# Log-sum-exp over rows: the early store cut into fifteen transfers of unequal partition counts

## Chip, cores and metric

The kernel runs on one core of a Trainium2 chip. The metric is device time in microseconds (us); the figure for a kernel is the median of its runs.

## The reference

```python
def setup_inputs():
    batch, seq, dim = 32, 512, 1024
    return {"x": np.random.randn(batch, seq, dim).astype(np.float32)}

def reference(x):
    max_x = np.max(x, axis=-1, keepdims=True)
    return (max_x.squeeze(-1) + np.log(np.sum(np.exp(x - max_x), axis=-1))).astype(np.float32)
```

There are 16,384 rows of 1024 floats, 64 MB to be read, and one float per row, 64 KB, to be written.

## The kernel before

Each of the 128 partitions takes 128 rows of x, so the results form a tile `res` of 128 partitions by `NC` = 128 columns. The first `W` = 112 columns hold one block of the output (`out_rows`, 112 consecutive floats of each partition), the last `B` = 16 columns another (`out_rest`). The kernel takes the logarithm of the plain sum of exponentials without subtracting the maximum, and checks beside that that no sum went out of bounds; only if one did, a repair branch computes everything again with the maximum. With this input the branch isn't taken.

Eighteen loads, listed in `LOADS` from 16 rows per partition down to less than half a row, go into a ring of 48 rows per partition. They are issued on SyncE (SP) by `load` (L140), in order; SP waits before a load until the engines have let go of its part of the ring. All loads are issued well before the kernel's end, since the last ones find free space early. ScalarE (ACT) computes the exponentials of what has landed, in place (L230); the sums are formed on VectorE (DVE) (L241), on GpSimd (POOL) and DVE together (L235 and L172), or with a fused multiply-add of half rows near the end (L251). The last row comes in two pieces, whose sums ACT accumulates itself (L204).

When the first `LATE` = 119 rows per partition are summed, ACT computes the logarithm of the first 112 columns (`ln_early`, L270), between two of its exponentials. SP waits for that and issues the early store of these 112 columns (L278): one transfer of 128 partitions with 448 bytes each. It raises the semaphore `sp.sem`, called `early_store`, by 16 when it has landed.

After the last exponential, ACT computes the logarithm of the other 16 columns (L281, and L283 for the last one, which is `ln_last`). SP waits for it and issues the last store (L287), 128 partitions with 64 bytes each, on the semaphore `stored`. Beside these, DVE and TensorE (PE) finish the check (L292 to L310). At the end SP waits for `done`, which ACT and DVE raise after the check, then for the early store (L368) and for the last store (the instruction behind L369), and clears the semaphores. So the order on SP at the end is: wait for L270, early store, wait for L283, last store, waits for the end.

A transfer raises its semaphore by 16 in all. Transfers issued on SP stand in one queue, called q1 in the profile.

Of the kernel before, what the change touches and what calls it, by code (L numbers as in the profile page):

```python
# [16 lines left out]
B = 16  # L17
LATE = 119
AHEAD = 3

# [31 lines left out]
def kernel(  # L54
# [5 lines left out]
    nc = tc.nc  # L60
# [4 lines left out]
    P = nc.NUM_PARTITIONS  # L65
# [11 lines left out]
    W = NC - B  # L77
# [4 lines left out]
    out_rows = out_flat[0 : P * W].rearrange("(p c) -> p c", p=P)  # L82
    out_rest = out_flat[P * W : n].rearrange("(p c) -> p c", p=P)

    def source(e0, size):
        assert e0 >= W * d or e0 + size <= W * d
        return x_rest[:, e0 - W * d : e0 - W * d + size] if e0 >= W * d else x_rows[:, e0 : e0 + size]
# [8 lines left out]
    def sbuf(name, cols, dtype=fp32, rows=P):  # L96
        return nc.alloc_sbuf_tensor(name, [rows, cols], dtype).ap()
# [3 lines left out]
    res = sbuf("res", NC)  # L101
# [18 lines left out]
    sp = Counted(nc, nc.sync, "early_store")  # L120
# [14 lines left out]
    def load(i, here, done_before, size):  # L135
        for a, b, who, at in users:
            if a < here + size and b > here:
                sp.wait(who, at)
        users[:] = [u for u in users if not (u[0] < here + size and u[1] > here)]
        return nc.sync.dma_start(  # L140
            out=ring[:, here : here + size], in_=source(done_before, size)
        ).then_inc(landed[i], 16)
# [44 lines left out]
    for i, (size, ops) in enumerate(loads):  # L187
# [5 lines left out]
        dma = load(i, here, done_before, size)  # L193
        if i < AHEAD:
            first_loads.append(dma.ins)
# [3 lines left out]
        for k, (how, s) in enumerate(ops):  # L199
            rows = ring[:, p : p + s * d].rearrange("p (c d) -> p c d", d=d)  # L200
            if how in "YZ":
# [3 lines left out]
                    out=last_exp[:, here - p : end - p], in_=ring[:, here:end], func=AF.Exp,  # L205
# [10 lines left out]
            elif how == "A":  # L216
# [3 lines left out]
                    out=v, in_=v, func=AF.Exp, accum_out=sumexp[:, c : c + 1]  # L220
# [11 lines left out]
            if how == "F":  # L232
# [3 lines left out]
                    out=rows[:, :, 0:H], in0=rows[:, :, 0:H], in1=rows[:, :, H:d], op=ALU.add  # L236
                ))
                folded.append((c, s, p, at))
            elif how == "R":
                dve.wait(act, at)  # L240
                who = (dve, dve.did(nc.vector.reduce_sum(  # L241
                    out=sumexp[:, c : c + s], in_=rows, axis=AX.X
                )))
                users.append((p, p + s * d, *who))
            elif how == "T":
# [3 lines left out]
                for r in range(s):  # L249
                    lo = rows[:, r, 0:H]  # L250
                    who = (dve, dve.did(nc.vector.scalar_tensor_tensor(  # L251
                        out=lo, in0=lo, scalar=1.0, in1=rows[:, r, H:d],
# [13 lines left out]
            if c == LATE:  # L266
# [4 lines left out]
                    out=res[:, 0:W], in_=sumexp[:, 0:W], func=AF.Ln  # L271
# [3 lines left out]
                early_act = summed_by_act  # L275
        assert here == end
    sp.wait(act, ln_early)
    nc.sync.dma_start(out=out_rows, in_=res[:, 0:W]).then_inc(sp.sem, 16)  # L278

    act.wait(dve, dve.n)  # L280
    act.did(nc.scalar.activation(out=res[:, W:LAST], in_=sumexp[:, W:LAST], func=AF.Ln))  # L281
# [2 lines left out]
        out=res[:, LAST:NC], in_=last_sum, func=AF.Ln, bias=sumexp[:, LAST:NC]  # L284
# [8 lines left out]
        out=clamped[:, LATE:NC], in0=sumexp[:, LATE:NC], scalar=LOW,  # L293
# [10 lines left out]
        out=over[:, 0:half], in0=last_piece[:, 0:half], scalar=CEILING,  # L304
# [15 lines left out]
            read.then_inc(done, 1)  # L320
    with nc.If(all_fine < 1):

        nc.scalar.wait_ge(sp.sem, 16)
        nc.scalar.wait_ge(stored, 16)
        rows = 0
        steps = 0
        for c0 in range(0, NC, RING):
            s = min(RING, NC - c0)
            v = ring[:, 0 : s * d].rearrange("p (c d) -> p c d", d=d)
            neg = clamped[:, c0 : c0 + s]  # L330
            if c0:
                nc.scalar.wait_ge(ready, steps)
            edge = max(c0, min(W, c0 + s))
            for c1, c2 in ((c0, edge), (edge, c0 + s)):
                if c1 == c2:
                    continue
                nc.scalar.dma_start(
                    out=ring[:, (c1 - c0) * d : (c2 - c0) * d],
                    in_=source(c1 * d, (c2 - c1) * d),
                ).then_inc(again, 16)  # L340
                rows += 16
            nc.vector.wait_ge(again, rows)
            nc.vector.tensor_reduce(
                out=neg, in_=v, op=ALU.max, axis=AX.X, negate=True
            ).then_inc(ready, 1)
            nc.vector.wait_ge(ready, steps + 1)
            nc.vector.tensor_add(
                out=v, in0=v, in1=neg[:, :, None].to_broadcast([P, s, d])
            ).then_inc(ready, 1)
            nc.scalar.wait_ge(ready, steps + 2)  # L350
            nc.scalar.activation(out=v, in_=v, func=AF.Exp).then_inc(ready, 1)
            nc.vector.wait_ge(ready, steps + 3)
            nc.vector.reduce_sum(
                out=sumexp[:, c0 : c0 + s], in_=v, axis=AX.X
            ).then_inc(ready, 1)
            steps += 4
        nc.scalar.wait_ge(ready, steps)
        nc.scalar.activation(out=res, in_=sumexp[:, 0:NC], func=AF.Ln).then_inc(ready, 1)
        nc.vector.wait_ge(ready, steps + 1)
        nc.vector.tensor_sub(out=res, in0=res, in1=clamped).then_inc(ready, 1)  # L360
        nc.scalar.wait_ge(ready, steps + 2)
        nc.scalar.dma_start(out=out_rest, in_=res[:, W:NC]).then_inc(again, 16)
        nc.scalar.dma_start(out=out_rows, in_=res[:, 0:W]).then_inc(again, 16)
        nc.scalar.wait_ge(again, rows + 32)

    nc.scalar.sem_inc(done, 1)
    nc.sync.wait_ge(done, 2)
    nc.sync.wait_ge(sp.sem, 16)  # L368
    nc.sync.sem_clear(range(landed[0].num, stored.num))  # L369
    kind = dict(sync_type="semaphore", id=stored.num, ant_name="stored")  # L370
    nc.sync.add_instruction(mybir.InstEventSemaphore(
# [54 lines left out]
```

## Time and profile before

| | |
|---|---|
| time, median of 3 runs | 161.67 us (161.55 to 161.7) |
| span of the profiled execution | 160.2 us |
| the difference of the two | 1.47 us |
| DVE busy | 114.2 us, 71% of the span |
| ACT busy | 114.5 us, 71% |
| POOL busy | 37.3 us, 23% |
| PE busy | 2.2 us, 1% |
| q1's packets | 97.8% of 16 engines' span |
| read from HBM, written to it | 67.11 MB, 0.07 MB |

The profile records one execution, and only its span; the time of a run also holds what lies before the span's first instruction and behind its last. Busy time doesn't count waiting, nor the issuing of DMAs, which shows only in SP's rows of the timeline (marked SPq). A row of the timeline has the start and the length in us, the engine, the line and the operation with its output and input. The span starts with the first load's issue.

### The profile page before, as it was taken

What the parts mean: (1) busy time and instruction counts of PE and PEld (TensorE: products, weight loads), DVE (VectorE), ACT (ScalarE), POOL (GpSimd) and SP (SyncE); (2) the same over time, 40 slices, a digit from 0 to 9 for tenths busy, and PEclk for the clock granted to TensorE, in tenths of its full rate; (3) what the DMA queues carried; (4) which work ended last, traced back from release to release, by engine and by line L of the source; (5) the groups of instructions that cost most, each with busy time, mean ns of one, the idle gap of its engine ahead of it and who ended that gap; (6) DMA issues with size and microseconds to landing.
All of it is one profiled execution on the core that took longest, in us unless ns stands there. A gap on an engine that the chain in (4) does not pass through costs nothing.

```text
span 160.2 us, 219 instructions
## 1 busy us (share of the span) xinstructions
PE 2.2 (1%) x26; PEld 1.1 (1%) x26; DVE 114.2 (71%) x59; ACT 114.5 (71%) x31; POOL 37.3 (23%) x11
## 2 busy tenths in 40 slices
PE   0000000000000000000000000000000000000022
PEld 0000000000000000000000000000000000000011
DVE  0000000009999499994999859959999999999996
ACT  3000059990799709995099949992999989799996
POOL 0000000000000000000000994690004969891000
DMA  7996996996996996996999999999999999999992
GB/s 262 524 524 262 524 524 262 524 524 262 524 524 262 524 507 278 524 491 295 483 442 442 442 425 409 409 409 471 423 405 426 458 409 393 450 413 425 411 411 102
DMA packets 2881, 67.18 MB, mean 419 GB/s; under 512 B 576, under 2 KB 704, under 8 KB 1344
## 3 DMA queue, kind: packets, MB, share of 16 engines
q1 hardware_dynamic: 2880, 67.18, 97.8%
q14 instruction: 1, 0.01, 0.0%
HBM read 67.11 MB, written 0.07 MB: 419 GB/s over the span
## 4 chain that ended last, share of the span: by engine, by line
DMA 52%; ACT 28%; DVE 19%; issue 1%; SPq 0%; PE 0%
DMA ring<-in_x_dram 52%; ACT ring L230 28%; DVE sumexp L241 16%; DVE sumexp L172 2%; DVE ring L251 1%; SPq L140 0%; DVE over L303 0%; PE count L308 0%; ACT res L270 0%; DVE clamped L292 0%; DVE fine L310 0%; DVE sumexp L214 0%
## 5 line engine op out<-in xcount | busy, mean ns | idle before, releaser
L230 ACT ACTIVATE ring<-ring 128x16384 f32<-128x16384 f32 (+16 forms) x23 | 111.7, 4909 | 41.9 <-DMA ring<-in_x_dram 41.9
L241 DVE TENSOR_REDUCE sumexp<-ring 128x16 f32<-128x16384 f32 (+4 forms) x9 | 85.6, 9512 | 41.6 <-ACT ring L230 41.6
L235 POOL TENSOR_TENSOR ring<-ring 128x3072 f32<-128x3072 f32 (+3 forms) x7 | 37.1, 5311 | 107.2 <-ACT ring L230 107.2
L172 DVE TENSOR_REDUCE sumexp<-ring 128x6 f32<-128x3072 f32 (+3 forms) x7 | 18.4, 2655 | 0.0
L251 DVE SCALAR_TENSOR_TENSOR ring<-ring 128x512 f32<-128x512 f32 x15 | 9.6, 688 | 0.4 <-ACT ring L230 0.4
L126 ACT ACT_TABLE_LOAD x1 | 1.3, 1283 | 2.4 <-PEq L63 2.4
L157 PE MATMUL count<-far,bad 128*1 128x1 f32 x2 | 0.2, 164 | 153.0 <-DVE clamped L152 153.0
L127 DVE MEMSET ones<- 128x1 f32 x1 | 0.1, 59 | 2.5 <-PEq L63 2.5
L161 PE MATMUL count<-sumexp,ones 128*1 128x1 f32 x18 | 1.6, 164 | 3.6 <-DVE ring L251 3.6
L251 DVE DVE_READ_ACCUMULATOR ring<-ring 128x1 f32 x15 | 1.2, 83 | 0.0
L204 ACT ACTIVATE last_exp<-ring 128x544 f32<-128x544 f32 (+1 forms) x2 | 1.2, 585 | 0.0
L157 PEld LDWEIGHTS count<-far,bad 128*1 128x1 f32 x2 | 0.1, 80 | 153.0 <-DVE clamped L152 153.0
L161 PEld LDWEIGHTS count<-sumexp,ones 128*1 128x1 f32 x18 | 0.8, 81 | 4.5 <-DVE ring L251 4.5
L303 DVE SCALAR_TENSOR_TENSOR over<-ring 128x240 f32<-128x240 f32 x1 | 0.4, 404 | 0.0
L310 DVE TENSOR_SCALAR fine<-count 1x1 int32<-1x1 f32 x1 | 0.1, 146 | 0.3 <-PE count L308 0.3
L152 DVE SCALAR_TENSOR_TENSOR clamped<-clamped,sumexp 128x119 f32<-128x119 f32 x1 | 0.3, 282 | 0.0
L270 ACT ACTIVATE res<-sumexp 128x112 f32<-128x112 f32 x1 | 0.3, 279 | 0.0
L283 ACT ACTIVATE res<-last_sum,sumexp 128x1 f32<-128x1 f32 x1 | 0.3, 261 | 0.0
L204 ACT ACTIVATION_READ_ACCUMULATOR last_exp<-ring 128x1 f32 x2 | 0.3, 126 | 0.0
L147 DVE TENSOR_SCALAR clamped<-sumexp 128x119 f32<-128x119 f32 x1 | 0.2, 221 | 0.0
L281 ACT ACTIVATE res<-sumexp 128x15 f32<-128x15 f32 x1 | 0.2, 208 | 0.0
L292 DVE SCALAR_TENSOR_TENSOR clamped<-sumexp 128x9 f32<-128x9 f32 x1 | 0.2, 169 | 0.0
(17 smaller groups left out, 1.8 us busy)
## 6 DMA issues: line engine op xcount, KB each, us to landing
ring<-in_x_dram SPq DMA_DIRECT2D x1, 6912.0 KB, 23.9
ring<-in_x_dram SPq DMA_DIRECT2D x1, 6400.0 KB, 19.7
ring<-in_x_dram SPq DMA_DIRECT2D x1, 4608.0 KB, 15.9
ring<-in_x_dram SPq DMA_DIRECT2D x1, 3584.0 KB, 24.0
ring<-in_x_dram SPq DMA_DIRECT2D x1, 3072.0 KB, 19.1
ring<-in_x_dram SPq DMA_DIRECT2D x1, 2288.0 KB, 24.1
ring<-in_x_dram SPq DMA_DIRECT2D x1, 1664.0 KB, 20.9
ring<-in_x_dram SPq DMA_DIRECT2D x1, 1264.0 KB, 23.6
```

What stands on the lines that cost most here:

```text
L126: nc.scalar.preload_act_table_set("natural_log_exp_and_others")
L152: dve.did(nc.vector.scalar_tensor_tensor(out=clamped[:, 0:LATE], in0=clamped[:, 0:LATE], scalar=0.0, in1=sumexp[:, 0:LATE], op0=ALU.bypass ...
L157: pe.did(nc.tensor.matmul(count, lhsT=bad[:, 0:1], rhs=far, start=True, stop=False))
L161: return pe.did(nc.tensor.matmul(count, lhsT=ones, rhs=sumexp[:, c : c + 1], **kw))
L172: at = dve.did(nc.vector.reduce_sum(out=sumexp[:, c0 : c0 + s0], in_=halves, axis=AX.X))
L204: at = act.did(nc.scalar.activation(out=last_exp[:, here - p : end - p], in_=ring[:, here:end], func=AF.Exp, accum_out=first_sum if how == ...
L230: at = act.did(nc.scalar.activation(out=v, in_=v, func=AF.Exp))
L235: at = pool.did(nc.gpsimd.tensor_tensor(out=rows[:, :, 0:H], in0=rows[:, :, 0:H], in1=rows[:, :, H:d], op=ALU.add))
L241: who = (dve, dve.did(nc.vector.reduce_sum(out=sumexp[:, c : c + s], in_=rows, axis=AX.X)))
L251: who = (dve, dve.did(nc.vector.scalar_tensor_tensor(out=lo, in0=lo, scalar=1.0, in1=rows[:, r, H:d], op0=ALU.mult, op1=ALU.add, accum_out ...
L270: ln_early = act.did(nc.scalar.activation(out=res[:, 0:W], in_=sumexp[:, 0:W], func=AF.Ln))
L303: dve.did(nc.vector.scalar_tensor_tensor(out=over[:, 0:half], in0=last_piece[:, 0:half], scalar=CEILING, in1=last_piece[:, half : 2 * half ...
```

## The change

The early store is issued as fifteen transfers in a row, over 15, 14, 13 and so on down to 2 partitions, which makes 119, and over the last 9. Each carries the 448 bytes of each of its partitions and raises `sp.sem` by 16, so that the two waits for the early store count to 240. Nothing else differs.

```diff
+PIECES = (15, 14, 13, 12, 11, 10, 9, 8, 7, 6, 5, 4, 3, 2, 9)
...
     sp.wait(act, ln_early)
-    nc.sync.dma_start(out=out_rows, in_=res[:, 0:W]).then_inc(sp.sem, 16)
+    edge = 0
+    for size in PIECES:
+        nc.sync.dma_start(
+            out=out_rows[edge : edge + size], in_=res[edge : edge + size, 0:W]
+        ).then_inc(sp.sem, 16)
+        edge += size
+    assert edge == P
...
-        nc.scalar.wait_ge(sp.sem, 16)
+        nc.scalar.wait_ge(sp.sem, 16 * len(PIECES))
...
-    nc.sync.wait_ge(sp.sem, 16)
+    nc.sync.wait_ge(sp.sem, 16 * len(PIECES))
```

## The prediction

> **What bounds the kernel now.** I read the page's first lines and its chain of waits, then SP's own rows in the timeline (SP carries both stores), then what SP waits for, and then the DMA issues.
>
> ```profile
> span 160.2 us, 219 instructions
> DMA 52%; ACT 28%; DVE 19%; issue 1%; SPq 0%; PE 0%
> ```
>
> Loading, exponentials and sums alternate along the whole span; SP's issuing is 0% of the chain. So the change, which adds nothing but DMA issues on SP after the last load was issued, can act only at the very end, through the store that follows it there.
>
> ```profile
> 136.82 2.23 SPq L140 DMA_DIRECT2D ring<-in_x_dram  x1
> 150.28 0.28 ACT L270 ACTIVATE res<-sumexp 128x112 f32<-128x112 f32 x1
> 150.59 0.35 SPq L278 DMA_DIRECT2D out_dram<-res  x1
> 158.48 0.26 ACT L283 ACTIVATE res<-last_sum,sumexp 128x1 f32<-128x1 f32 x1
> 158.77 0.34 SPq L287 DMA_DIRECT2D out_dram<-res  x1
> 158.95 0.15 DVE L310 TENSOR_SCALAR fine<-count 1x1 int32<-1x1 f32 x1 [0.28 <-PE count L308]
> ...
> SPq L278 <- ACT res L270: 11.5, 1, 11.5
> SPq L287 <- ACT res L283: 7.8, 1, 7.8
> ...
> out_dram<-res SPq DMA_DIRECT2D x1, 56.0 KB, 7.4
> out_dram<-res SPq DMA_DIRECT2D x1, 8.0 KB, 1.4
> ```
>
> Columns are start, us, engine and line; below them what SP waited for, and KB and us from issue to landing. The early store (L278) starts at 150.59, 11.5 us after SP last had something to do. It lands at 150.59 + 7.4 = 158.0. SP then stands idle 7.8 us for the last logarithm (L283) and issues the last store (L287) at 158.77. That lands at 158.77 + 1.4 = 160.2, which is the span's end; the other branch to the end, DVE's check at L310, is over at 158.95 + 0.15 = 159.1. So the last store's issue time sets the end one for one, and the early store has 158.77 - 150.59 = 8.18 us of SP's time and 2.2 us of landing time to spare.
>
> The span is 160.2 us and the median of the runs 161.67 us. The 1.47 us between them lie outside the span, and I leave them as they are: predicted time = 161.67 + the shift of the span's end.
>
> **What the change removes and adds.** One issue goes and fifteen come, all on SP, all behind one wait for L270. Each reads a few partitions of the same tile, so bytes and rows written are the same (128 rows of 448 bytes). The loads keep their issue times, since the last of them (136.82) is off SP's hands at 139.05, and they stand ahead of the pieces in the queues. ACT, DVE, POOL and PE get no new instruction. Two waits count to 240 instead of 16; the one in the repair branch isn't reached with this input. SP's last wait for the early store (L368) now waits for fifteen landings. Behind the fifteen issues, on SP, stands exactly one thing that counts: the last store.
>
> *SP's time.* The nearest prices are the loads' issues, in batches without a wait between them:
>
> ```profile
> 126.46 0.33 SPq L140 DMA_DIRECT2D ring<-in_x_dram  x1
> 126.83 0.43 SPq L140 DMA_DIRECT2D ring<-in_x_dram  x1
> 126.83 1.41 SPq L140 DMA_DIRECT2D ring<-in_x_dram  x3
> 135.50 0.33 SPq L140 DMA_DIRECT2D ring<-in_x_dram  x1
> 135.87 0.91 SPq L140 DMA_DIRECT2D ring<-in_x_dram  x2
> L140 SPq DMA_DIRECT2D ring<-in_x_dram x18: 327/428/2229, 0.0 to 136.8; - x18
> ```
>
> The last row, all eighteen issues of L140, gives min/median/max in ns. The first issue of a batch, which comes out of a wait, takes 0.33 us; the ones right behind it take 0.43, 0.10 more, with a gap of 0.04 (126.46 + 0.33 to 126.83). So a train of fifteen at these prices is 0.35 + 0.04 + 14 x 0.47 = 6.97 us: it ends at 157.56, with 1.21 us to spare. That spare is 0.086 us for each of the fourteen followers, a fifth of one issue's time. At 0.33 us for every follower it would end at 156.15, with 2.62 us to spare.
>
> But every row is an issue of 128 partitions, and a piece is another kind of transfer. The packet counts show what all twenty transfers of this kernel have in common:
>
> ```profile
> DMA packets 2881, 67.18 MB, mean 419 GB/s; under 512 B 576, under 2 KB 704, under 8 KB 1344
> ```
>
> Packets under 512 bytes are the two stores' 2 x 128 rows and 320 more, 16 for each of 18 loads and 2 stores: every transfer ends with one small packet per engine, and these bring its semaphore to 16. A piece of 15 or fewer rows can't be cut over 16 engines in equal shares, so SP must find another split for each piece, and the increments that engines without a row don't post must come from somewhere. Fifteen pieces with 128 rows on at most 128 engine shares leave at least 15 x 16 - 128 = 112 of 240 increments to be made up. Both are work inside the issue that no row shows. Bounds: below, nothing or less (fewer rows to lay out, down to 0.33 us per issue, which isn't a floor either); above, 2.23 us, the dearest issue seen, which stood in a stall. The only extra step that rows price is the 0.10 between an issue out of a wait and one right behind another. I take one such step for the other split and one for the missing increments: 0.43 + 0.21 = 0.64 us, nearer to the batch rows than to the stalled one.
>
> Sum: 150.59 + 0.35 + 0.04 + 14 x (0.64 + 0.04) = 160.50 for the moment when the last store can be issued, instead of 158.77: 1.73 us later. As a follower it would take 0.43 rather than 0.34: 0.09 more. Together 1.8 us, 163.5 us.
>
> The Trainium skill, "DMA: Bandwidth & Descriptors", section "Why a DMA increments its semaphore by 16 and not by 1", says that such a transfer runs on the largest number of engines up to 16 that divides the row counts, on the lowest-numbered ones, and that the issuing sequencer itself writes the increments which the others don't post. "Perfetto Trace Analysis", section on HWDGE DMA instructions, puts that write inside the issue's recorded time. No run here shows either yet; neither page prices it on this chip, and by them alone the train could be anything from 6.97 us up.
>
> *The engines' time.* A piece puts packets on few engines. If rows go to the lowest engines one each, the first one gets 15 rows and 15 increments, 30 packets instead of 9.
>
> ```profile
> DMA packets 26, 0.01 MB, mean 10 GB/s; under 512 B 26, under 2 KB 26, under 8 KB 26
> q1 hardware_dynamic: 26, 0.01, 3.8%
> ...
> DMA  0000000000000000000026655310000000000000
> DMA packets 144, 0.01 MB, mean 7 GB/s; under 512 B 144, under 2 KB 144, under 8 KB 144
> ```
>
> The first two rows are the window 157.3 to 158.2, where only the early store's tail is left: 3.8% of 16 engines' 0.9 us over 26 packets is 21 ns each. The other two are 159.0 to 160.2, the last store: its 144 packets begin in the slice at 159.0 + 20 x 0.03 = 159.60, 0.83 us behind the issue. Thirty packets take 0.63 us on the fullest engine; from 157.3, since when no packet of a load is left (all 26 are under 512 bytes), that is over at 157.9. Cover: 159.6 - 157.9 = 1.7 us, so I cost this at nothing. If pieces are issued late (the forecast), they also reach the engines late, but still ahead of the last store by SP's order.
>
> **The rivals.** *No change* (not slower). The train fits: an issue of a piece costs below 0.52 us, and the 8.18 us of SP's idle time swallow all of it. For it: the eighteen load issues have a median of 0.43 us and a least of 0.33, whatever their size, and a piece has at most 15 rows to lay out instead of 128. Against: a spare of 0.086 us per piece is little for two new steps. It decides where a piece's issue ends below 0.52 us. Time 161.7.
>
> *The pieces queue up on one engine.* If an engine holds its next row back until the increment before it is confirmed, the first engine runs fifteen row-and-increment pairs one after the other. The last store's packets are over in the slice at 159.84 and it lands at 160.17: 0.33 us for a confirmation. Fifteen of these from 157.3 end at 162.25; the last store's packets would start there instead of 159.60, 2.65 us later: 164.3 us. It decides from 2.3 / 15 = 0.15 us per pair.
>
> ```profile
> 156.00:157.00 1.00, 0.38 (x4) 0.17 (x4) 0.94 (x3) 1.00 (x2) 0.00 (x0) 1.00 1.02 393
> ```
>
> Against it: from 156 to 157 the engines were busy at a share of 1.02, though loads ended in it, each with an increment, and those left no gap. But the loads write on chip, and the pieces write to HBM. In the same section the skill states that the increment lands only after all earlier writes of its engine; by the bounds above that is between nothing and 2.65 us here.
>
> *A limit on transfers in flight.* The 2.23 us issue is a stall:
>
> ```profile
> DMA packets 1344, 59.60 MB, mean 429 GB/s; under 512 B 144, under 2 KB 144, under 8 KB 144
> ...
> DMA packets 1783, 64.47 MB, mean 428 GB/s; under 512 B 192, under 2 KB 192, under 8 KB 247
> ...
> 118.93 19.09 DMA ring<-in_x_dram
> ...
> ring<-in_x_dram SPq DMA_DIRECT2D x1, 1264.0 KB, 23.6
> ring<-in_x_dram SPq DMA_DIRECT2D x1, 928.0 KB, 25.4
> ring<-in_x_dram SPq DMA_DIRECT2D x1, 240.0 KB, 21.0
> ```
>
> The packet rows count those begun by 139.05, when it ended, and by 150.59. Eighteen loads have 18 x 144 = 2592, so 1248 were waiting, 78 an engine, when SP was let go, and 809, 51 an engine, when the early store comes. If the limit is on waiting packets, the pieces stay below 78, since each adds at most 2 to an engine while the loads drain: no cost. If it is on transfers, ten were in flight at 136.82: the 3072 KB load that landed at 138.02, those of 2288, 1664, 1264, 928, 672, 496, 368 and 272 KB, and the 240 KB one itself. SP went on 1.03 us after that landing. At 150.59 six loads are in flight: the 1264 KB one, issued at 126.83, has landed at 150.4, the 928 KB one, issued 0.47 later, lands at 152.7, the 240 KB one at 157.8. Four pieces then go at once, six more as loads land, the tenth at 157.8 + 1.03 = 158.8, the other five 0.47 apart: the last store at 161.3, 2.5 us late, 164.2 us. It decides once more than ten are in flight.
>
> *Faster*: no row shows a gain, but the engines stay at work until shortly before the last store, whose 0.83 us to the first packet come after some 2 us without packets; were that start quicker, up to 0.4 us could go: 161.3.
>
> **How the numbers follow.** Chances: issue train too long 0.40, no change 0.30, one engine's queue 0.11, limit on transfers 0.11, faster 0.08. A difference of 0.2%, 0.32 us, is about what a measurement of this kernel can tell from no change. So slower 0.62, same 0.30, faster 0.08. The forecast is that of the likeliest, 163.5. Its own range is 161.9 (0.54 us a piece) to 167.0 (0.88 us a piece: 150.98 + 14 x 0.92 = 163.9, 5.1 late, and 0.1). The range over all cases reaches down to the no-change case less a tenth of a percent, 161.4, and up to 167.0, which holds the two queue rivals too. Faster by more, and pieces dearer than 0.88 us, are left out.
>
> **What would show it.** In the profile after, SP's rows should have fifteen L-rows of `out_dram`, the first at 150.6, followers about 0.64 us long, and the last store's issue at 160.5, with SP's wait for L283 gone from its list. Right behind the train and not at 158.77 is the sign of the forecast. Followers of 0.5 us or less with the last store still at 158.77 and 1.4 to landing mean no change. A last store at 158.77 but with more than 1.4 us to landing means the engine's queue. Pieces that start at the loads' landings, with stalls of a microsecond in between, mean the limit. Loads, ACT and DVE should stand where they are to 0.1 us; if they move, all of this is wrong.

## The result and the profile after

The changed kernel takes 162.22 us, the one before 161.68 us beside it: a ratio of 1.0032, interval 1.0023 to 1.0041, 0.54 us slower. The forecast was 163.5 us in a range of 161.4 to 167.0: the direction is right, but the size, 1.8 us, was more than three times too large, and the step that should have made it did not happen.

The new lines shift the numbers: the pieces are issued at L281, the last logarithm is L290, the last store L294, and SP's last wait for the early store L375. Here are the page's first line and DMA row, then SP's rows of the timeline and the groups of its two lines (min/median/max in ns, then first and last start):

```profile
span 160.9 us, 233 instructions
DMA packets 2993, 67.18 MB, mean 418 GB/s; under 512 B 688, under 2 KB 816, under 8 KB 1456
...
150.53 5.37 SPq L281 DMA_DIRECT2D out_dram<-res  x15
158.71 0.36 SPq L294 DMA_DIRECT2D out_dram<-res  x1
...
L281 SPq DMA_DIRECT2D out_dram<-res x15: 253/297/423, 150.5 to 155.6; - x15
L294 SPq DMA_DIRECT2D out_dram<-res x1: 361/361/361, 158.7 to 158.7; - x1
```

The train of fifteen took 5.37 us and was over at 155.90. A piece's issue took 0.30 us in the median (0.25 to 0.42), not 0.64, and less than a load's 0.43. The last store was issued at 158.71, even 0.06 earlier than before. What SP waited for (us in total, times, longest), and the last store's row among the DMA issues (KB, us from issue to landing):

```profile
SPq L294 <- ACT res L290: 2.8, 1, 2.8
SPq L375 <- DMA out_dram<-res: 1.6, 1, 1.6
...
out_dram<-res SPq DMA_DIRECT2D x1, 8.0 KB, 2.1
```

SP stood idle 2.8 us before the last store (7.8 in the kernel before), so the train cost nothing. The last store, however, took 2.1 us to land instead of 1.4, and SP waited 1.6 us at the end for the early store, a wait that was not there before. That is the whole loss: 0.7 us between the two profiled spans, 160.2 and 160.9, and 0.54 us between the medians of the runs. The loads, ACT and DVE stand where they stood, to 0.1 us. The packets that begin from 157.5 to 158.5 us, and those from 159 us on:

```profile
DMA packets 0, 0.00 MB, mean 0 GB/s; under 512 B 0, under 2 KB 0, under 8 KB 0
...
DMA  0000000000036520000000000000000000000000
DMA packets 144, 0.01 MB, mean 4 GB/s; under 512 B 144, under 2 KB 144, under 8 KB 144
```

Each of the forty slices of the second window is 0.05 us. The last store's 144 packets begin at 159 + 11 x 0.05 = 159.55, 0.84 us behind the issue, as before. All packets of the early store, those of 4 bytes that carry its increments too, had begun by 157.5. So it is not data that is late, but the arrival of increments. The trace also records each increment of a semaphore when it arrives. The last ones of the early store (E) and some of the last store's (L), in us:

```
before  E: ... 157.90 157.96 157.98            L: 160.01 ... 160.13 160.14 160.18
after   E: ... 160.32 160.47 160.48 160.51 160.66  L: 160.01 ... 160.28 160.49 160.65 160.70 160.84
```

After the change, twelve of the last store's sixteen increments arrive by 160.28, and four from 160.49 to 160.84: behind the pieces' increments.

The trace has 143 updates of the early store's semaphore: fifteen, one for each piece, about 0.13 us after the end of its issue, and 128 from 157.48 on, from the engines. So a piece of k rows ran on k engines, and SP made up the other 16 - k in one step. The packets under 512 bytes say the same: 688 - 576 = 112 more, 128 increments instead of 16.

### The profile page after: what moved, and what is told of

Its sections match the earlier page's. It is cut to its first block, busy times and chain, and to the rows that moved or that the text cites. A ratio compares the mean times of both kernels' runs of the same rounds, so it can differ in the third digit from the quotient of the medians.

```text
span 160.9 us, 233 instructions
## 1 busy us (share of the span) xinstructions
PE 2.2 (1%) x26; PEld 1.1 (1%) x26; DVE 114.3 (71%) x59; ACT 114.5 (71%) x31; POOL 37.3 (23%) x11
## 4 chain that ended last, share of the span: by engine, by line
DMA 52%; ACT 28%; DVE 18%; issue 1%; SPq 0%; PE 0%
DMA ring<-in_x_dram 52%; ACT ring L231 27%; DVE sumexp L242 15%; DVE sumexp L173 2%; DVE ring L252 1%; SPq L141 0%; DVE over L310 0%; PE count L315 0%; ACT res L271 0%; DVE clamped L299 0%; DVE fine L317 0%; DVE sumexp L215 0%
## 5 line engine op out<-in xcount | busy, mean ns | idle before, releaser
L290 ACT ACTIVATE res<-last_sum,sumexp 128x1 f32<-128x1 f32 x1 | 0.3, 261 | 0.0
```

## The experiments

The theory, A: an engine that has increments of several transfers to post puts some 0.2 us between two of them, whatever their rows. The time is then set by the number of transfers on the fullest engine, which here is fifteen if every piece uses that engine, and the last store's increment on it is the sixteenth. Rivals: B, any further issue or transfer costs its share; C, the uneven load of the engines, or the number of packets, costs.

The pieces are issued 0.36 us apart, which is more than 0.2. They become a burst because they stand behind the loads: the first was issued at 150.53, but no increment of an engine arrives before 157.48, when the last load is landing (157.73).

Each ratio below is to the kernel before, run beside the experiment. Each block first shows the edit to the changed kernel, then what was expected.

**Eight pieces of 16 partitions.**

```diff
-PIECES = (15, 14, 13, 12, 11, 10, 9, 8, 7, 6, 5, 4, 3, 2, 9)
+PIECES = (16,) * 8
```

> Eight pieces of 16 partitions: eight transfers, each of which can use all 16 engines with one row and one increment each. Theory A (each increment on an engine waits until the row written to HBM before it is confirmed, some 0.21 to 0.23 us, so the time is set by the number of early transfers on the fullest engine): the fullest engine posts its eighth increment at 157.5 + 7 x 0.23 = 159.1, before the last store's increments are due at 160.0, so the span stays at 160.2 and the time at that of before, within 0.1 us. Theory B (any cutting of the early store costs, in proportion to the number of issues, 0.6 us for fourteen more): 7/14 of it, +0.3 us.

The time is 161.72 us, ratio 1.0004 (0.9995 to 1.0013): no change. SP's rows, and the last store's landing:

```profile
SPq L294 <- ACT res L290: 4.6, 1, 4.6
SPq L375 <- DMA out_dram<-res: 0.2, 1, 0.2
...
L281 SPq DMA_DIRECT2D out_dram<-res x8: 361/420/421, 150.7 to 153.9; - x8
...
out_dram<-res SPq DMA_DIRECT2D x1, 8.0 KB, 1.4
```

The early store's last increment came at 159.45, before the last store's first at 160.14, and that one's landing is 1.4 us again. B's share of 0.3 us isn't there. The issues are dearer than the changed kernel's, 0.42 us, though with hardly more rows, 16 each: see below.

**Fifteen transfers by columns.**

```diff
-PIECES = (15, 14, 13, 12, 11, 10, 9, 8, 7, 6, 5, 4, 3, 2, 9)
+PIECES = (8,) * 7 + (7,) * 8
...
-            out=out_rows[edge : edge + size], in_=res[edge : edge + size, 0:W]
+            out=out_rows[:, edge : edge + size], in_=res[:, edge : edge + size]
...
-    assert edge == P
+    assert edge == W
```

> Fifteen transfers again, but each over all 128 partitions and 8 or 7 of the 112 columns: the work is even over the engines, every engine gets fifteen increments and 120 short rows. Theory A: fifteen increments on every engine, so +0.6 us as with the change, or some tenths more for the rows. Theory C (the unevenness is what costs, the lowest engines being overloaded with packets): nothing is uneven, no change to before. SP's train of fifteen at 0.43 us and a gap of 0.04 ends at 157.6, 1.1 us before the last store, on any theory.

The time is 162.88 us, ratio 1.0072 (1.0059 to 1.0086): slower than the changed kernel, though nothing is uneven. So unevenness isn't the cost, and neither are the increments that SP makes up, since all 240 come from engines here. Theory A has the sign; its +0.6 us and "some tenths more" were 1.19 us.

```profile
L281 SPq DMA_DIRECT2D out_dram<-res x15: 348/432/588, 150.6 to 157.4; - x15
...
SPq L375 <- DMA out_dram<-res: 1.8, 1, 1.8
SPq L294 <- ACT res L290: 1.1, 1, 1.1
```

The 240 increments arrived from 157.56 to 161.00, one every 14 ns: 0.23 us between two of the same engine while all sixteen are at it. No packet began from 158.8 to 159.6, so the rows were over while 2 us of increments were still to come; whether the many rows of 28 to 32 bytes slowed the earlier ones, this run doesn't tell.

**Twenty-three transfers, sixteen of them of one partition.**

```diff
-PIECES = (15, 14, 13, 12, 11, 10, 9, 8, 7, 6, 5, 4, 3, 2, 9)
+PIECES = (16,) * 7 + (1,) * 16
```

> Seven pieces of 16 partitions and sixteen of one: 23 transfers, 23 rows and 23 increments on the fullest engine, all others have seven. Theory A: its last early increment at 157.5 + 22 x 0.23 = 162.5 and the last store's one 0.18 behind, +2.4 us against before, 0.29 us for each transfer beyond the twelfth or so. Theory B: 22/14 of 0.6 us, +0.9 us. If only rows or packets count (21 ns each): 46 packets take 1.0 us, over at 158.4, no change.

The time is 163.52 us, ratio 1.0113 (1.0097 to 1.0128), +1.83 us. B's 0.9 and the packets' nothing are both out; A's 2.4 was too much, because it took 0.23 us for every step. The last increments here are those of one engine alone:

```
early store  159.44 159.68 159.88 160.06 160.24 160.43 160.61 160.79 160.98 161.16 161.34 161.53 161.71 161.89
last store   (fifteen by 160.24)                                                                        162.08
```

Alone, an engine posts one every 0.18 us, and the last store's sixteenth increment is the next in that row, 0.18 us behind, while its other fifteen had arrived 1.8 us earlier. SP's last wait and the landing:

```profile
SPq L294 <- ACT res L290: 0.3, 1, 0.3
...
out_dram<-res SPq DMA_DIRECT2D x1, 8.0 KB, 3.3
```

The 23 issues just fitted: 0.3 us of SP's idle time was left.

**The same fifteen as loads.**

```diff
+    spare = sbuf("spare", W)
...
+    nc.sync.dma_start(out=out_rows, in_=res[:, 0:W]).then_inc(sp.sem, 16)
     edge = 0
     for size in PIECES:
         nc.sync.dma_start(
-            out=out_rows[edge : edge + size], in_=res[edge : edge + size, 0:W]
+            out=spare[edge : edge + size, :], in_=x_rows[edge : edge + size, 0:W]
...
-    nc.sync.wait_ge(sp.sem, 16 * len(PIECES))
+    nc.sync.wait_ge(sp.sem, 16 * (1 + len(PIECES)))
```

> The early store in one transfer again, and behind it fifteen loads of 15 down to 2 and 9 partitions with 448 bytes each from x into a tile that nothing reads, on the same semaphore: sixteen transfers with the same engines and sizes as with the change, but written on chip. Theory A in the form that it is the confirmation from HBM that each increment waits for: the loads' increments follow each other within some 30 ns, no change to before. Theory A in the form that any small transfer costs an engine 0.2 us: +0.8 us.

The time is 162.54 us, ratio 1.0050 (1.0036 to 1.0064), +0.85 us. So it is not a confirmation of a write to HBM, for these transfers write on chip: the first form of A, which is how I had argued it in the prediction, is refuted, the second holds at its 0.8 us. The last increments follow each other by about 0.18 us here too (160.58, 160.76, 160.94, 161.13).

**Sixteen pieces of eight partitions.**

```diff
-PIECES = (15, 14, 13, 12, 11, 10, 9, 8, 7, 6, 5, 4, 3, 2, 9)
+PIECES = (8,) * 16
```

> Sixteen pieces of eight partitions. In all 128 increments, as many as with eight pieces of sixteen, but sixteen on each of eight engines instead of eight on each of sixteen. Theory A1 (an engine posts its next increment 0.18 us or more after its last): sixteen in a row on an engine, from 157.5 + 15 x 0.18 = 160.2 to, at 0.23, 160.9, the last store's one 0.18 behind: +0.2 to +0.9 us. Theory A2 (all engines' increments pass one place, some 14 ns each, and nothing else holds them): 128 x 14.8 ns = 1.9 us, done at 159.4, no change.

The time is 162.70 us, ratio 1.0065 (1.0052 to 1.0079), +1.0 us, where eight pieces of sixteen with the same 128 increments cost nothing. A2 falls as the only limit; the loss is at A1's upper end, a tenth above it. Half of the last store's increments arrived from 160.17 to 160.28, the other half from 160.75 to 161.35: those of the eight engines that the pieces used. Late in the train these eight posted in rounds 0.21 us apart (at 160.29, 160.50, 160.72 and 160.92). So all sixteen pieces ran on the same eight engines; that pieces of other sizes share their engines in this way is read from the number of late increments, four after the change, one with the pieces of one partition.

**A semaphore for each piece.**

```diff
+    early = [nc.alloc_semaphore(f"early{i}") for i in range(len(PIECES))]
...
-    for size in PIECES:
+    for i, size in enumerate(PIECES):
...
-        ).then_inc(sp.sem, 16)
+        ).then_inc(early[i], 16)
...
-    nc.sync.wait_ge(sp.sem, 16 * len(PIECES))
+    for sem in early:
+        nc.sync.wait_ge(sem, 16)
```

> The changed kernel with a semaphore of its own for each of the fifteen pieces, and fifteen waits of 16 at the end. If the increments hold each other up because they all update one semaphore, those of one engine come closer than 0.1 us and the time goes back to that of before. If it is the engine that waits between two increments, whatever their target (A1), the last store still lands at 160.8, +0.5 us as with the change.

The time is 162.43 us, ratio 1.0051 (1.0038 to 1.0065), no better than the changed kernel. The last increments of the first six semaphores came at 158.23, 158.40, 158.57, 158.75, 158.92 and 159.09: again 0.17 us apart, on as many semaphores. It is the engine that spaces them, not the semaphore. This kernel has more waits at its end, so its time isn't to be set against the changed kernel's to the tenth.

**The last store on ACT's queue.**

```diff
-    sp.wait(act, ln_last)
-    nc.sync.dma_start(out=out_rest, in_=res[:, W:NC]).then_inc(stored, 16)
+    act.wait(act, ln_last)
+    nc.scalar.dma_start(out=out_rest, in_=res[:, W:NC]).then_inc(stored, 16)
```

> The changed kernel with the last store issued by ACT, on the other queue, so that its descriptors don't stand behind the pieces in SP's queue. If the order is that of a queue, all sixteen increments of the last store land within 0.2 us of each other, at about 160.2, and the early store's last one at 160.66 sets the end: +0.4 to +0.5 us. If an engine orders the increments of all its queues, those of the last store on the low engines still land behind the pieces' ones, at 160.8, +0.5 to +0.6 us: the landing tells these apart, the time hardly.

The time is 162.24 us, ratio 1.0035 (1.0022 to 1.0049). The last store's landing:

```profile
out_dram<-res ACTq DMA_DIRECT2D x1, 8.0 KB, 2.2
```

Twelve of its increments arrived by 160.24, the others at 160.34, 160.54, 160.72 and 160.99, the last one 0.19 us behind the early store's last at 160.80. The order holds across queues: it belongs to the engine. The Trainium skill, "DMA: Bandwidth & Descriptors", section "Queues, rings and completion order", says that the increment is a strongly ordered write that lands after all earlier writes of its engine, across its queues; this run agrees.

**127 partitions and one.**

```diff
-PIECES = (15, 14, 13, 12, 11, 10, 9, 8, 7, 6, 5, 4, 3, 2, 9)
+PIECES = (127, 1)
```

> Two pieces, of 127 partitions and of one. 127 is prime, so all 128 rows go to one engine if the split must divide, with two increments. Theory A1 (increments count, rows cost their 21 ns): the rows take 2.7 us from 157.3 to 160.0, two increments by 160.2, and the last store's share on that engine goes behind them, 0.1 for eight short rows and 0.18 for its increment: 160.5, +0.2 to +0.3 us. If every row waited as a row with its increment does, 128 x 0.2 = 26 us, +23 us. If 127 rows are spread over the engines after all, no change.

The time is 162.48 us, ratio 1.0053 (1.0039 to 1.0066), +0.8 us where A1 had 0.2 to 0.3: the sign, not the size. The trace has four updates of the semaphore: two from SP, one at 160.73 from 127 rows on one engine, one at 160.91. The rows' packets began from 157.04 to 160.10, 24 ns apart: rows don't wait for each other, only increments do (0.18 us again; the last store's late one came at 161.10). The expectation left out a lag of 0.6 us from the end of the rows to the increment.

```profile
L281 SPq DMA_DIRECT2D out_dram<-res x2: 324/3256/6187, 150.8 to 151.2; - x2
```

The second piece's issue stood for 6.19 us, with eight transfers in flight. The number of transfers isn't what holds SP up, for the changed kernel issued its last piece with eighteen in flight and didn't stall. The backlog of one engine would fit; no run tests it.

**Eleven and thirteen pieces.**

```diff
-PIECES = (15, 14, 13, 12, 11, 10, 9, 8, 7, 6, 5, 4, 3, 2, 9)
+PIECES = (15, 15, 15, 14, 14, 13, 12, 10, 9, 7, 4)
...
+PIECES = (15, 14, 13, 13, 12, 11, 10, 9, 9, 8, 7, 5, 2)
```

> Eleven pieces of unequal partition counts, the largest 15 and the smallest 4, so that the first engine gets eleven increments. Theory A1 with 0.20 to 0.23 us between two increments of the fullest engine: the eleventh at 157.5 + 10 x 0.225 = 159.75, the last store's next one at 159.95, before 160.0: no change to before. If every piece costs its share of the fifteen's 0.5 us: +0.35 us.

> Thirteen pieces of 15 down to 2 partitions: thirteen increments on the first engine. Theory A1: the thirteenth at 157.5 + 12 x 0.225 = 160.2, the last store's one at 160.4, against 160.18 without pieces: +0.2 us. If every piece costs its share of the fifteen's 0.5 us: +0.45 us.

The times are 161.75 us, ratio 1.0006 (0.9997 to 1.0015), and 161.87 us, ratio 1.0015 (1.0006 to 1.0024), +0.24 us. Both are as A1 had them, and against the equal shares of 0.35 and 0.45 us. The eleven are not quite free of it, though:

```profile
SPq L375 <- DMA out_dram<-res: 1.1, 1, 1.1
...
out_dram<-res SPq DMA_DIRECT2D x1, 8.0 KB, 1.6
```

The early store's last increment came at 160.21, not at A1's 159.75, and the last store's sixteenth at 160.39, again 0.19 us behind, after fifteen by 160.18. So the queue already reaches the last store here; what it costs is too little for the times to tell from nothing. In the order of the fullest engine's early increments:

| early transfers | on the fullest engine | ratio to before |
|---|---|---|
| 8, of 16 partitions | 8, on all engines | 1.0004 |
| 11 | 11 | 1.0006 |
| 13 | 13 | 1.0015 |
| 15, the change | 15 | 1.0032 |
| 15, by columns | 15, on all engines | 1.0072 |
| 16, of 8 partitions | 16, on eight engines | 1.0065 |
| 23 | 23, on one engine | 1.0113 |

Up to eleven no cost shows in the time, then it rises; where more engines have equally long rows of increments at the same time, each goes slower (0.21 us on eight engines, 0.23 on sixteen, instead of 0.18) and the rise is steeper.

## Why the prediction was wrong

**The frame was right.** Only the last store's path counted; loads, ACT and DVE stayed. The last store's landing was named as a place to look, and the sign "a last store at 158.77 but with more than 1.4 us to landing" is what came, 158.71 and 2.1. That the kernel came out slower, as forecast, is luck: the step that the forecast rested on did nothing, and another one made a smaller loss.

**The step that failed** is SP's time: "one such step for the other split and one for the missing increments: 0.43 + 0.21 = 0.64 us". Fifteen issues took 5.37 us, 0.36 each with the gap, and the term of 1.73 us is nothing. The 0.10 us by which an issue behind another is dearer than one out of a wait was no price for such a step. Right behind another, an issue's time goes with the number of engines that it feeds: 0.42 us for 16 partitions and 0.43 for 128 (16 engines both), 0.35 for 14, 0.30 for 8, 0.25 for one or two. The rows of the second piece (14 partitions) and of the fourteenth (2), and the group of the sixteen pieces of 8:

```profile
150.99 0.35 SPq L281 DMA_DIRECT2D out_dram<-res  x1
...
155.32 0.25 SPq L281 DMA_DIRECT2D out_dram<-res  x1
...
L281 SPq DMA_DIRECT2D out_dram<-res x16: 289/295/368, 150.7 to 155.8; - x16
```

Fewer engines save more than the 16 - k made up in one go cost. Only the first piece, which comes out of a wait, was dearer than what it replaced, 0.42 us against 0.35. The direction of the effect was within the bounds that I gave ("below, nothing or less"), and the value taken was at the wrong end.

**The term taken at nothing**, the engines' time, is where the loss is: "Thirty packets take 0.63 us on the fullest engine ... so I cost this at nothing". The packets do fit, and all had begun by 157.5. But the arrival of an increment isn't a packet of 21 ns: from the first at about 157.5 the fullest engine needs 0.18 to 0.23 us for each, 160.66 for the fifteenth and 160.84 for the last store's, against 160.18 before: 0.66 us.

**The rival was right in its main step**, "the pieces queue up on one engine", which had a chance of 0.11, with 0.33 us for a pair taken from one confirmation. Measured are 0.18 to 0.23, and the point from which it decides, 0.15, was passed by little; so 0.5 and not 2.65 us. Two parts of it were wrong: that the last store's packets would start late (they start on time; its increments are late), and that it takes a write to HBM. The argument against it, that loads end without a gap, proved nothing: their increments on an engine are 0.6 us and more apart, because the rows between take that long, so the spacing never showed.

**No limit on transfers**: the fifth piece would have had to wait for a landing at 152.7 and 1.03 us more; it was issued at 152.19, and the longest issue of the train was 0.42 us.

**Small slips in the sums**, on which nothing rests: by the prediction's own sum 0.54 us a piece gives 162.1 and not 161.9, and 0.88 us gives 166.9 and not 167.0; the slice in which the last store's packets end is over at 159.81, not 159.84.

**Open**: what the engine waits for in its 0.18 us. It isn't a write to HBM, a shared semaphore, the rows' count or SP's queue; whether it is the increment's own acknowledgement or that of the row before it, which no run here separates, isn't settled. Nor is the 14 ns between increments of all sixteen engines together, and why each is slower in company.

## What to carry to other kernels

Count a transfer not only by its bytes and its issue, but by the increments that it leaves on each engine: after a burst of small transfers an engine posts one increment in about 0.2 us, and the next transfer's completion stands in that row, even from another queue, though its packets ran on time. Transfers that are issued further apart than that still form a burst when they wait behind a backlog, as the pieces did behind the loads. Where a store that ends the kernel follows such a burst, compare the number of transfers on the fullest engine times 0.2 us with the time from the burst's start until that store lands, here from 157.5 to 160.2: eight cost nothing, eleven nothing that the times show, and fifteen 0.5 us. Pieces behind an idle queue were not run.

## What the runs showed of the hardware

- The time of an issue right behind another goes with the engines that it feeds, 0.25 us for one, 0.42 for sixteen, and hardly with its rows (16 or 128).
- A transfer of 127 partitions ran on one engine, its rows one after the other for 3.1 us, and the issue behind it stood for 6.19 us.
- Two increments of one engine that has several to post arrive 0.17 to 0.19 us apart where one engine's row can be followed, 0.21 where eight engines post equally long rows, and 0.23 where sixteen do; behind the loads, whose increments on an engine are 0.6 us and more apart anyway, this doesn't show.
- An increment stands behind the earlier ones of its engine even when its transfer was issued on another queue (0.19 us behind the pieces' last).
